# A hybrid decoder layer on one core: the output projection of the first 512 tokens between the SSD's chunks

## The chip, the cores and the metric

The kernel runs on one core of a Trainium2 chip. The core has TensorE (matmuls and transposes, "PE" in the rows, its weight loads "PEld"), VectorE ("DVE"), ScalarE ("ACT"), GpSimd ("POOL") and SyncE ("SP"), which issues the DMAs. Each engine works through its own queue in order and waits on semaphores for the others. The metric is the device time of one execution, in microseconds, as the median of several runs.

## The reference

One layer of a decoder for a prompt of 2048 tokens and, with the same weights, 32 sample tokens (8 sequences of 4). The input projection feeds four parallel groups of 256 channels each, whose normed outputs are concatenated, projected and added to x; then comes a feed-forward block.

```python
xn = rmsnorm(x, P['norm_mix_g'][l])
u, q, k, v, fr, z, xbc, dtr, sb, sc, sh = split_cols(xn @ P['w_in'][l])
ya, h_s5n = s5_mix(u, ...)                                    # diagonal state-space model
yb = fox_prompt(q, k, v, logf)                                # attention, 4 heads of 64
yc, h_ssdn, buf_ssdn = ssd_mix(z, xbc, dtr, ...)              # chunks of 128 tokens
yd, buf_scn = short_conv_mix(sb, sc, sh, buf_sc, P['sc_conv_w'][l])
# ya, yb, yc, yd each go through rmsnorm
x = x + jnp.concatenate([ya, yb, yc, yd], axis=-1) @ P['w_out'][l]
hn = rmsnorm(x, P['norm_ffn_g'][l])
x = x + jnp.square(jax.nn.relu(hn @ P['w_up'][l])) @ P['w_down'][l]
```

The shapes are `D_MODEL` 1024, `SEQ` 2048, `FFN_WIDTH` 4096; outputs are y, the keys, values and states of both groups.

## The kernel before, in words

Prompt tokens are handled in 16 tiles of 128 and 4 blocks of 512. Numbers that need more than 16 bits are held as a high and a low half (`w[:, k, 0]`, `w[:, k, 1]`), so that one product of 128 tokens with 256 columns is 8 x 3 = 24 matmuls (`proj_tok`), accumulated in PSUM.

The stages are traced by `run`. `phase_in` norms and projects the input and runs the S5, the short convolution and the sample's attention. Then come the SSD (`ssd`), the attention of the prompt (`fox`), the output projection (`outproj`) and the feed-forward block (`ffn`). A scheduler orders the instructions of each engine by priority and readiness; `priority(bg)` places attention ahead of the SSD (`priority(first)`), and both ahead of `outproj`, so a stage of lower priority fills the gaps of a higher one. A wait between stages follows from which tile was traced as written before which read.

Attention works by query block j (512 tokens) and head h: `maxima` runs ahead and finds row maxima (scores into a PSUM bank, `mx` on VectorE at L871); `attend` goes through 4j + 4 key blocks: two score matmuls, the exponential on ScalarE (`P`, L902), its high half `ph` (ScalarE or VectorE), its low half `pl` (GpSimd, L909), and 12 matmuls with `v`. A head ends with `fo_o` (VectorE, L920). After four heads `fox_out` norms the block's four tiles: a square on ScalarE, a power on GpSimd, a scale on ScalarE, two transposes on TensorE, a split into `fo_cat`, a DMA into the DRAM buffer `catD[1][j]`. It uses PSUM tag `b` (5 banks).

The SSD goes through 16 chunks: `prepare` (decay matrix `sE`, transposes, `G`), `advance` (products into `y`, state `shT`, gate `syo`), then `fox_out` of the chunk before into `catD[2]`. It uses tag `x` (the 2 banks named `px`) and tag `d` (1 bank, `pd`). Between chunks the sample's SSD (`sample`) goes on by one step, and `w_out` prepares one quarter of the output weights in chunks 10, 12, 13 and 14: a 1 MB load, a square pass (L183) and a high half (L176) on ScalarE, a low half (L177) on VectorE, and the scale between them.

`outproj` uses `px` for products and `pd` for transposes. It takes tokens 0 to 511 (block 0), 512 to 1023, then blocks 2 and 3. For each half block it loads `cat` (the four groups) and `x2` (the input), runs 8 products of 512 columns, adds each in two halves (L1908), norms the sum (`norm_pair`), and for blocks 0 and 1 stores the sum to `xD` and the normed parts to `hD` in DRAM; the FFN reads these back later. The sample's 32 tokens go through `out_sample` (192 matmuls `px<-catS,w`) after the first half block. Its tiles lie in pools that are opened after the SSD's pools are closed.

Of the kernel before, what the change touches and what calls it, by code (L numbers as in the profile page):

```python
# [9 lines left out]
F32 = mybir.dt.float32  # L10
F16 = mybir.dt.float16
# [3 lines left out]
OP = mybir.AluOpType  # L15
# [4 lines left out]
D = 1024  # L20
# [7 lines left out]
BLOCKS = [(2, 3), (0, 1)]  # L28
FC = 256
# [74 lines left out]
class K:  # L104
# [131 lines left out]
    def run(self):  # L236
        tc = self.tc
        with ExitStack() as ctx:
# [9 lines left out]
            self.wp = ctx.enter_context(self.pool("wp", 4))  # L248
            first = tc.cur_priority
            tc.cur_priority = first + 50000  # L250
            if "ssd" in self.stages:
                with self.priority(first), self.banks(t="x", s="x", o="d"), ExitStack() as c3:
                    self.mark("ssd")
                    self.ssd(c3)
            if "fox" in self.stages:
                with self.priority(bg):
                    self.mark("fox")
                    self.fox(mix)
            if getattr(self, "dump", None):
                self.dump_cat()  # L260
# [786 lines left out]
    def ssd_prompt(self, ctx, Dp, av, sample):  # L1047
# [109 lines left out]

        hT, yo = None, None
        self.Wo, wo = [], self.w_out()
        nx = prepare(0)  # L1160
        for i in range(NT):
            cur, nx = nx, prepare(i + 1) if i + 1 < NT else None
            old = yo
            hT, yo = advance(i, hT, *cur)

            if old is not None:
                self.fox_out(p2, old, 128, i - 1, "t", 2)
            next(sample, None)
            if i in (10, 12, 13, 14):
                next(wo)  # L1170
        for _ in sample:
            pass
# [703 lines left out]

    def outproj(self, ctx, mix):

        nc, A = self.nc, self.A
# [7 lines left out]

        self.xD = {b: [self.dr.tile([128, 2 * D], F32, name=f"x2D{b}{i}") for i in range(2)] for b in BLOCKS[1]}
# [21 lines left out]
        for b in BLOCKS[1]:  # L1910
            hns = [rot.tile([128, 7, 4, 2, N2[b]], F16, name="hnr") for _ in range(2)]
            for i, hn in enumerate(hns):
                cat, x2 = load(2 * b + i, BLOCKS[0][0], i)
                for t in range(2):
                    for m in (0, 2):
                        product(cat, x2, t, m)
                self.norm_pair(x2, gb, hn[:, :, :, :, 0:128])
                if i == 0 and N2[b] > 128:
                    self.out_sample(g8, [h[:, :, :, :, 128:] for h in hns])
                nc.sync.dma_start(self.xD[b][i], x2.rearrange("p t d -> p (t d)"))  # L1920
                nc.sync.dma_start(self.hD[b][i], hn.rearrange("p o k a n -> p (o k a n)"))
# [396 lines left out]
```

## Time and profile before

| | us |
|---|---|
| median of 3 runs (lowest, highest) | 2579.73 (2573.97, 2580.62) |
| the profiled execution | 2576.48 |
| its span, first to last instruction | 2574.7 |
| TensorE busy in the span | 2422.8 |
| VectorE busy | 1855.7 |
| ScalarE busy | 1209.2 |
| GpSimd busy | 980.4 |

A row of the trace gives an instruction's start and length on its engine; the idle time before it is put down to what ended it. Matmuls are pipelined, so each is shown longer than the distance to the next one; the pace is read from a run of them. The granted clock is the mean of TensorE's clock over a stretch, as a share of 2.4 GHz; the clock has that level and 1.2 GHz. Attention runs from about 740 to 1132 us, the SSD beside it from about 840 to 1030 us, and the feed-forward block from about 1290 us to the end.

### The profile page before, as it was taken

What the parts mean: (1) busy time and instruction counts of PE and PEld (TensorE: products, weight loads), DVE (VectorE), ACT (ScalarE), POOL (GpSimd) and SP (SyncE); (2) the same over time, 40 slices, a digit from 0 to 9 for tenths busy, and PEclk for the clock granted to TensorE, in tenths of its full rate; (3) what the DMA queues carried; (4) which work ended last, traced back from release to release, by engine and by line L of the source; (5) the groups of instructions that cost most, each with busy time, mean ns of one, the idle gap of its engine ahead of it and who ended that gap; (6) DMA issues with size and microseconds to landing.
All of it is one profiled execution on the core that took longest, in us unless ns stands there. A gap on an engine that the chain in (4) does not pass through costs nothing.

```text
span 2574.7 us, 51102 instructions
## 1 busy us (share of the span) xinstructions
PE 2422.8 (94%) x20496; PEld 1655.2 (64%) x20496; DVE 1855.7 (72%) x3636; ACT 1209.2 (47%) x2339; POOL 980.4 (38%) x1141
## 2 busy tenths in 40 slices
PE   7989998999999899999969999999999999999996
PEld 6975554444467677689846666666666666666663
DVE  7566667875576777655579898888886776777765
ACT  6434333033346677653455556555554333333333
POOL 3403121223124566651165555555534222222222
PEclk9999999999999998999979999999999999999998
DMA  6333415869732433347233443435466232232221
GB/s 178 100 76 95 90 41 194 306 245 345 239 110 81 134 97 103 103 147 248 79 122 133 147 172 143 156 138 178 156 260 234 107 123 84 101 123 104 81 78 68
DMA packets 201864, 368.42 MB, mean 143 GB/s; under 512 B 43829, under 2 KB 161714, under 8 KB 179322
## 3 DMA queue, kind: packets, MB, share of 16 engines
q1 hardware_dynamic: 187594, 293.29, 34.4%
q0 software_dynamic: 9376, 67.64, 7.2%
q10 hardware_dynamic: 4656, 4.23, 0.5%
q8 instruction: 160, 2.62, 0.4%
q14 instruction: 78, 0.64, 0.1%
HBM read 245.87 MB, written 116.39 MB: 141 GB/s over the span
## 4 chain that ended last, share of the span: by engine, by line
PE 63%; DVE 11%; POOL 8%; DMA 8%; ACT 4%; issue 4%; SPq 2%; POOLq 0%; DVEq 0%; ACTq 0%
PE pb L140 30%; PE px L140 28%; DMA ws<-in_w_up_dram 3%; PE pd L140 2%; DVE x L2203 2%; DVE wu L177 2%; PE pb L144 1%; DMA kp<-in_cache_v_dram,ptV 1%; ACT wdT L176 1%; POOL ht L2159 1%; DVE s5cat L480 1%; POOL ht L2157 1%; DVE wd L177 1%; PE pd L144 1%; POOL fr L2149 1%
## 5 line engine op out<-in xcount | busy, mean ns | idle before, releaser
L2203 DVE SCALAR_TENSOR_TENSOR x<-pb,ff,x 128x512 f32<-128x512 f32 x840 | 593.6, 744 | 107.0 <-PE pb L140 101.4
L140 PEld LDWEIGHTS <-wu 128*128 128x128 f16 x5376 | 524.6, 98 | 192.3 <-issue 20.0
L140 PE MATMUL px<-hn,wu 128*128 128x256 f16 (+1 forms) x3072 | 414.5, 275 | 12.3 <-DVE hn L1983 7.0
L140 PEld LDWEIGHTS <-ht 128*128 128x128 f16 x2712 | 263.7, 98 | 242.8 <-issue 23.4
L140 PE MATMUL pb<-wdT,ht 128*128 128x512 f16 x1440 | 378.9, 380 | 10.1 <-DVE x L2203 5.0
L140 PE MATMUL px<-xT,w 128*128 128x512 f16 (+1 forms) x1968 | 369.3, 339 | 1.5 <-ACT da L731 1.2
L140 PE MATMUL pb<-wd,ht 128*128 128x512 f16 x1272 | 330.0, 380 | 10.5 <-DVE x L2203 10.2
L140 PE MATMUL pb<-hn,wu 128*128 128x256 f16 (+1 forms) x2304 | 305.4, 276 | 6.5 <-ACT hn L1982 4.7
L140 PEld LDWEIGHTS <-w 128*128 128x128 f16 x2160 | 170.2, 99 | 188.0 <-issue 27.5
L2157 POOL TENSOR_TENSOR ht<-fr,ht 128x512 f16<-128x512 f32 (+1 forms) x60 | 80.8, 1347 | 402.7 <-ACT ht L2156 401.7
L909 POOL TENSOR_TENSOR pl<-P,ph 128x512 f16<-128x512 f32 (+3 forms) x160 | 166.8, 1052 | 154.3 <-ACT ph L906 64.8
L140 PE MATMUL px<-w,cat 128*128 128x256 f16 x1536 | 175.9, 273 | 3.0 <-DMA cat<-cat 3.0
L140 PE MATMUL px<-w,xT 128*128 128x128 f16 (+1 forms) x2400 | 158.9, 227 | 8.9 <-DVE v L576 3.3
L140 PEld LDWEIGHTS <-xT 128*128 128x128 f16 (+1 forms) x2672 | 155.8, 102 | 14.4 <-issue 4.2
L140 PEld LDWEIGHTS <-cat 128*128 128x128 f16 x1536 | 149.2, 98 | 22.7 <-DMA cat<-cat 3.1
L2131 ACT ACTIVATE fr<-fr 128x256 f32<-128x256 f32 (+1 forms) x192 | 78.0, 416 | 153.8 <-DVE fr L2112 152.4
L902 ACT ACTIVATE P<-pb,nck,cc 128x512 f32<-128x512 f32 (+3 forms) x160 | 113.0, 713 | 73.2 <-PE pb L140 67.5
L2154 ACT ACTIVATE ht<-fr 128x1024 f16<-128x1024 f32 (+1 forms) x60 | 64.2, 1070 | 137.6 <-POOL fr L2160 137.6
L871 DVE TENSOR_REDUCE mx<-pb 128x1 f32<-128x512 f32 (+3 forms) x160 | 94.8, 607 | 38.0 <-PE pb L140 36.6
L2132 ACT ACTIVATE fr<-fr 128x256 f32<-128x256 f32 (+1 forms) x256 | 104.1, 416 | 5.1
L177 DVE SCALAR_TENSOR_TENSOR wu<-ws,wsc,wu 128x1024 f16<-128x1024 f32 x64 | 91.2, 1432 | 13.3 <-ACT wu L176 13.1
L176 ACT ACTIVATE wu<-ws,wsc 128x1024 f16<-128x1024 f32 x64 | 64.8, 1039 | 64.9 <-POOL ws L2045 37.6
(717 smaller groups left out, 4196.0 us busy)
## 6 DMA issues: line engine op xcount, KB each, us to landing
w0D<-wu SPq DMA_DIRECT2D x16, 1792.0 KB
wu<-w0D SPq DMA_DIRECT2D x16, 1792.0 KB
ws<-in_w_up_dram SPq DMA_DIRECT2D x16, 1024.0 KB
ws<-in_w_down_dram SPq DMA_DIRECT2D x16, 1024.0 KB
w1D<-wd SPq DMA_DIRECT2D x16, 1024.0 KB
wd<-w1D SPq DMA_DIRECT2D x16, 1024.0 KB
w2D<-wdT SPq DMA_DIRECT2D x15, 1024.0 KB
wdT<-w2D SPq DMA_DIRECT2D x15, 1024.0 KB
```

The costliest lines, as they stand in the source:

```text
L140: self.nc.tensor.matmul(out, lhsT, rhs, start=start, stop=stop, skip_group_check=True)
L144: self.nc.tensor.transpose(out, in_, self.ident[:n, :n])
L176: self.nc.scalar.activation(hi, x, AF.Copy, scale=sc)
L177: self.nc.vector.scalar_tensor_tensor(lo, x, sc, hi, op0=OP.mult, op1=OP.subtract)
L871: nc.vector.tensor_reduce(mx[:, ii, jb:jb + 1], s[:, :n], axis=AX.X, op=OP.max)
L902: nc.scalar.activation(P[:, :n], s[:, :n], AF.Exp, bias=nck[:, j, h, kt:kt + 1], scale=cc[:, h // 2:h // 2 + 1])
L909: (nc.gpsimd if 1 else nc.vector).tensor_sub(pl[:, :n], P[:, :n], ph[:, :n])
L2131: nc.scalar.activation(x, x, AF.Relu)
L2132: nc.scalar.activation(x, x, AF.Square)
L2154: nc.scalar.activation(ht[:, o:o + m, 0, :], x, AF.Copy)
L2157: nc.gpsimd.tensor_sub(ht[:, 0:2, 1, :], C[:, 0:2, :], ht[:, 0:2, 0, :])
L2203: nc.vector.scalar_tensor_tensor(o, p, f, o, op0=OP.mult, op1=OP.add)
```

## The change

- `fox` is traced ahead of `ssd`; their priorities stay. So the SSD's loop can read `catD[1][0]`, attention's output for block 0.
- `w_out` runs in chunks 1 to 4.
- `out_tile(EARLY, t)` is the output projection of one tile of 128 tokens of block 0: it loads `ecat` and `ex2` (pool `eo`, two buffers), runs four products of 256 columns in the SSD's `px` banks, adds each into `ex2`, and stores the sum to `xD`. From chunk 6 on, two of these 16 quarters are traced behind each chunk.
- `outproj` skips the products of block 0 and reads the sum back from `xD` for the norm.

```diff
--- before.py
+++ after.py
@@ -26,6 +26,7 @@
 BIG = float(2.0 ** 100)
 S14 = float(2.0 ** -14)
 BLOCKS = [(2, 3), (0, 1)]
+EARLY = 0
 FC = 256
 PLAIN = ((0, 15), (1, 15))
 V_EARLY, V_LAG = 12, 4
@@ -246,16 +247,19 @@
                 bg = self.phase_in(c2)
             self.wst = ctx.enter_context(self.pool("wst", 2))
             self.wp = ctx.enter_context(self.pool("wp", 4))
+
+            self.xD = {b: [self.dr.tile([128, 2 * D], F32, name=f"x2D{b}{i}") for i in range(2)] for b in BLOCKS[1]}
             first = tc.cur_priority
             tc.cur_priority = first + 50000
-            if "ssd" in self.stages:
-                with self.priority(first), self.banks(t="x", s="x", o="d"), ExitStack() as c3:
-                    self.mark("ssd")
-                    self.ssd(c3)
             if "fox" in self.stages:
                 with self.priority(bg):
                     self.mark("fox")
                     self.fox(mix)
+            if "ssd" in self.stages:
+                with self.priority(first), self.banks(t="x", s="x", o="d"), ExitStack() as c3:
+                    self.mark("ssd")
+                    self.eo = c3.enter_context(self.pool("eo", 2))
+                    self.ssd(c3)
             if getattr(self, "dump", None):
                 self.dump_cat()
             with self.banks(mm="x", t="d"):
@@ -1155,6 +1159,7 @@
                 nc.gpsimd.tensor_mul(yo, yt, z)
             return hN, yo
 
+        early = (s for t in range(4) for s in self.out_tile(EARLY, t))
         hT, yo = None, None
         self.Wo, wo = [], self.w_out()
         nx = prepare(0)
@@ -1166,9 +1171,14 @@
             if old is not None:
                 self.fox_out(p2, old, 128, i - 1, "t", 2)
             next(sample, None)
-            if i in (10, 12, 13, 14):
+            if 1 <= i < 5:
                 next(wo)
+            if i > 5:
+                for _ in range(2):
+                    next(early, None)
         for _ in sample:
+            pass
+        for _ in early:
             pass
         self.fox_out(p2, yo, 128, NT - 1, "t", 2)
         t = self.ps("t", [128, 2, 128])
@@ -1874,6 +1884,23 @@
             self.Wo.append((w, f))
             yield
 
+    def out_tile(self, b, t):
+
+        nc, A, W = self.nc, self.A, self.Wo
+        cat = self.eo.tile([128, 8, 2, 128], F16, name="ecat")
+        for g in range(4):
+            nc.sync.dma_start(cat[:, 2 * g:2 * g + 2], self.catD[g][b][:, :, :, t * 128:t * 128 + 128])
+        x2 = self.eo.tile([128, D], F32, name="ex2")
+        r = (4 * b + t) * 128
+        nc.sync.dma_start(x2, A["x_prompt"][0, r:r + 128, :])
+        for m in range(4):
+            p = self.ps("t", [128, 256])
+            self.proj_tok(p, cat, W[m][0], 0, 256)
+            o = x2[:, m * 256:(m + 1) * 256]
+            nc.vector.scalar_tensor_tensor(o, p, W[m][1], o, op0=OP.mult, op1=OP.add)
+            yield
+        nc.sync.dma_start(self.xD[b][t // 2][:, t % 2 * D:t % 2 * D + D], x2)
+
     def outproj(self, ctx, mix):
 
         nc, A = self.nc, self.A
@@ -1884,8 +1911,6 @@
 
         self.xp = {BLOCKS[0][0]: ctx.enter_context(self.pool("x2a", 1))}
         rot = mix.enter_context(self.pool("rot", 2, "right"))
-
-        self.xD = {b: [self.dr.tile([128, 2 * D], F32, name=f"x2D{b}{i}") for i in range(2)] for b in BLOCKS[1]}
         N2 = {BLOCKS[1][0]: 128 + NS // 4, BLOCKS[1][1]: 128}
         self.hD = {b: [self.dr.tile([128, 7 * 4 * 2 * N2[b]], F16, name=f"hnD{b}{i}") for i in range(2)] for b in BLOCKS[1]}
 
@@ -1910,14 +1935,18 @@
         for b in BLOCKS[1]:
             hns = [rot.tile([128, 7, 4, 2, N2[b]], F16, name="hnr") for _ in range(2)]
             for i, hn in enumerate(hns):
-                cat, x2 = load(2 * b + i, BLOCKS[0][0], i)
-                for t in range(2):
-                    for m in (0, 2):
-                        product(cat, x2, t, m)
+                if b == EARLY:
+                    x2 = self.xp[BLOCKS[0][0]].tile([128, 2, D], F32, name="x2", tag=f"x2{BLOCKS[0][0]}{i}")
+                    nc.sync.dma_start(x2.rearrange("p t d -> p (t d)"), self.xD[b][i])
+                else:
+                    cat, x2 = load(2 * b + i, BLOCKS[0][0], i)
+                    for t in range(2):
+                        for m in (0, 2):
+                            product(cat, x2, t, m)
+                    nc.sync.dma_start(self.xD[b][i], x2.rearrange("p t d -> p (t d)"))
                 self.norm_pair(x2, gb, hn[:, :, :, :, 0:128])
                 if i == 0 and N2[b] > 128:
                     self.out_sample(g8, [h[:, :, :, :, 128:] for h in hns])
-                nc.sync.dma_start(self.xD[b][i], x2.rearrange("p t d -> p (t d)"))
                 nc.sync.dma_start(self.hD[b][i], hn.rearrange("p o k a n -> p (o k a n)"))
         first = [load(2 * BLOCKS[0][0] + i, BLOCKS[0][0], i) for i in range(2)]
         for i, t, m in ((i, t, m) for i in range(2) for t in range(2) for m in (0, 2)):
```

How this moves TensorE's queue: of the 1536 matmuls `px<-w,cat` of the prompt's output projection, 240 stand ahead of attention's last matmul in the kernel before and 1296 behind it; in the changed kernel 384 (now with `ecat`) stand ahead and 1152 behind. The 192 small ones of the sample (`px<-catS,w`) stand ahead of it before and behind it now. The SSD's chunks, which in the kernel before end with head (3, 0), now reach to attention's end; heads (2, 1) to (3, 0) hold ten chunks before and six now, heads (3, 1) to (3, 3) none before and four now.

TensorE at the end of attention, before (the matmuls with `v` and `pl` are attention's; `os` is the sample's sum of squares, `w,cat` the projection):

```order
L140 MATMUL pb<-v_3_11130,ph 128x64
L140 MATMUL pd<-os,ones 128x32 x3
L140 LDWEIGHTS pl
L140 MATMUL pb<-v_3_11130,pl 128x65
L140 LDWEIGHTS cat
L140 MATMUL px<-w,cat 128x256
```

and now (`sXd,sBt` is the state of the last chunk, `fo_on` a norm's transposes, `fn_sq`, `fn_rs` the sample's norm, `shT` the final state, `catS,w` the sample's projection):

```order
L141 MATMUL pb<-v_3_9840,ph 128x64
L141 LDWEIGHTS pl
L141 MATMUL pb<-v_3_9840,pl 128x65
L141 MATMUL px<-sXd,sBt 128x128
L145 MATMUL px<-cst,fo_on 128x128 x2
L141 MATMUL px<-ones,fn_sq_16255 32x1 x2
L141 MATMUL px<-cst,fn_rs 128x32
L145 MATMUL px<-cst,fo_on 128x128 x2
L145 MATMUL px<-cst,shT 128x128 x2
L145 MATMUL pb<-cst,fo_on 128x128 x2
L141 LDWEIGHTS w
L141 MATMUL px<-catS,w 128x32
```

The projection behind attention's last matmul has given way to the last SSD chunk's and the norms' transposes.

VectorE between the ends of heads (1, 3) and (2, 0), before:

```order
L871 TENSOR_REDUCE mx<-pb 128x1
L908 CAST ph<-P 128x512
L871 TENSOR_REDUCE mx<-pb 128x1
L1115 TENSOR_TENSOR sX<-px,dt 128x256
L1152 TENSOR_TENSOR syt<-pd,acu 128x256
L871 TENSOR_REDUCE mx<-pb 128x1
L1154 TENSOR_TENSOR syt<-syt,pd 128x256
L871 TENSOR_REDUCE mx<-pb 128x1
L874 TENSOR_REDUCE nm<-mx 128x4
L1125 TENSOR_TENSOR sE<-sE,px 128x512
L875 TENSOR_SCALAR nm<-nm,sh 128x4
L908 CAST ph<-P 128x512
```

and now (`w<-ws,w_sc,w` is the low half of a quarter of w_out, `w_f` to `wo_f` the scales):

```order
L188 TENSOR_SCALAR w_f<-pd 128x1
L875 TENSOR_REDUCE mx<-pb 128x1
L156 TENSOR_SCALAR w_m<-w_f 128x1
L1119 TENSOR_TENSOR sX<-px,dt 128x256
L192 TENSOR_SCALAR w_sc<-w_m 128x1
L178 SCALAR_TENSOR_TENSOR w<-ws,w_sc,w 128x8x256
L193 RECIPROCAL w_inv<-w_sc 128x1
L875 TENSOR_REDUCE mx<-pb 128x1
L1129 TENSOR_TENSOR sE<-sE,px 128x512
L912 CAST ph<-P 128x512
L1883 TENSOR_TENSOR wo_f<-w_inv,isc 128x1
L875 TENSOR_REDUCE mx<-pb 128x1
```

Between the ends of heads (1, 2) and (2, 0) there are four such halves now and none before, and 28 of the maxima `mx<-pb` where there were 24.

SP from the second load of w_out on, before:

```order
L160 DMA ws<-in_w_out_dram 128x8x256
L857 DMA q_12681<-qk_2912 64x512
L848 DMA kbm<-kb 74x512
L848 DMA kba<-kb 74x512
L857 DMA q_12681<-qk_2912 64x512
L858 DMA q_12682<-qk_2912 64x512
L859 DMA q_12682<-row 10x512
```

and now:

```order
L161 DMA ws<-in_w_out_dram 128x8x256
L1892 DMA ecat<-cat_0_117 128x4x128
L1892 DMA ecat<-cat_0_121 128x4x128
L1892 DMA ecat<-cat_0_129 128x4x128
L1895 DMA ex_15190<-in_x_prompt_dram 128x1024
L1892 DMA ecat<-cat_0_117 128x4x128
L1892 DMA ecat<-cat_0_121 128x4x128
L852 DMA kba<-kb 74x512
L852 DMA kbm<-kb 74x512
```

Six loads of `ecat` and `ex2` stand ahead of attention's `kba` and `kbm`.

## Rows read from the trace of the kernel before

**Rows 1.** Busy time by engine, share of the span, instructions (the page).

```profile
PE 2422.8 (94%) x20496; PEld 1655.2 (64%) x20496; DVE 1855.7 (72%) x3636; ACT 1209.2 (47%) x2339; POOL 980.4 (38%) x1141
```

**Rows 2.** Stretches: length, busy us (instructions) by engine, granted clock, DMA share, GB/s.

```profile
785.90:848.90 63.00, 56.27 (x802) 44.59 (x799) 40.73 (x99) 43.99 (x100) 28.69 (x34) 0.95 0.36 103
848.90:909.10 60.20, 55.65 (x544) 41.44 (x543) 45.66 (x105) 41.66 (x102) 38.26 (x59) 1.00 0.43 124
909.10:987.20 78.10, 76.88 (x839) 58.59 (x837) 63.59 (x138) 57.10 (x115) 55.80 (x69) 1.00 0.37 106
987.20:1044.10 56.90, 50.94 (x435) 37.27 (x435) 41.21 (x99) 40.67 (x87) 36.49 (x46) 0.82 0.26 71
1044.10:1132.20 88.10, 82.55 (x1154) 64.26 (x1153) 49.68 (x94) 56.63 (x94) 54.77 (x52) 0.98 0.35 107
1132.20:1283.00 150.80, 150.80 (x1384) 136.23 (x1382) 80.55 (x138) 58.17 (x95) 27.48 (x38) 1.00 0.51 178
1283.00:1335.00 52.00, 29.60 (x220) 23.86 (x218) 41.13 (x46) 33.13 (x52) 30.98 (x25) 0.80 0.34 127
```

**Rows 3.** Timeline of VectorE, ends of heads: start, us, line, operation, tiles.

```profile
909.11 0.42 DVE L920 TENSOR_TENSOR fo_o<-pb,rl 128x256 f32<-128x256 f32 x1
...
987.22 0.41 DVE L920 TENSOR_TENSOR fo_o<-pb,rl 128x256 f32<-128x256 f32 x1
...
1044.14 0.42 DVE L920 TENSOR_TENSOR fo_o<-pb,rl 128x256 f32<-128x256 f32 x1
```

**Rows 4.** Chain of waits after attention, timeline of TensorE inside it: start, us, count.

```profile
1203.85 33.41 PE px L140 x306
...
1107.38 0.45 PE L140 MATMUL px<-catS,w 128*128 128x32 f16 x12
```

**Rows 5.** Groups: busy us, mean ns, idle before; three of 987.2:1044.1, last 760:1160.

```profile
L176 ACT ACTIVATE w<-ws,w_sc 128x2048 f16<-128x2048 f32 x3 | 6.0, 2013 | 0.0
...
L183 ACT ACTIVATE w<-ws 128x2048 f16<-128x2048 f32 x1 | 1.9, 1903 | 0.0
...
L177 DVE SCALAR_TENSOR_TENSOR w<-ws,w_sc,w 128x2048 f16<-128x2048 f32 x3 | 7.0, 2344 | 0.0
...
L871 DVE TENSOR_REDUCE mx<-pb 128x1 f32<-128x512 f32 (+3 forms) x146 | 88.6, 621 | 37.6 <-PE pb L140 36.3
```

**Rows 6.** Waits of TensorE in 987.2:1044.1: us in total, times, longest us.

```profile
PE pb L144 <- ACT fo_on L959: 3.4, 2, 2.6
```

**Rows 7.** Waits of TensorE in 1044.1:1132.2.

```profile
PE px L140 <- DMA cat<-cat: 3.0, 1, 3.0
PE pb L140 <- DMA kba<-kb: 2.5, 2, 2.1
```

**Rows 8.** Timeline, steps of a chunk's norm; the last row is another chunk's.

```profile
1009.97 0.42 DVE L1152 TENSOR_TENSOR syt<-pd,acu 128x256 f32<-128x256 f32 x1 [1.29 <-PE pd L140]
...
1010.43 0.42 DVE L1154 TENSOR_TENSOR syt<-syt,pd 128x256 f32<-128x256 f32 x1
...
1014.35 0.42 ACT L956 ACTIVATE fo_on<-syo 128x256 f32<-128x256 f32 x1
...
1014.65 0.21 ACT L956 ACTIVATION_READ_ACCUMULATOR fo_on<-syo 128x1 f32 x1
...
1014.95 0.19 POOL L150 TENSOR_SCALAR fo_rs<-fo_ssq 128x1 f32<-128x1 f32 x1
...
1015.99 0.56 POOL L151 TENSOR_TENSOR fo_rs<-fo_rs,mhalf 128x1 f32<-128x1 f32 x1
...
1016.70 0.54 ACT L959 ACTIVATE fo_on<-syo,fo_rs 128x256 f32<-128x256 f32 x1
...
1028.50 0.91 POOL L1155 TENSOR_TENSOR syo<-syt,sz 128x256 f32<-128x256 f32 x1
```

**Rows 9.** Timeline of SP, issues around the first w_out loads.

```profile
837.73 0.39 SPq L160 DMA_DIRECT2D ws<-in_w_out_dram  x1
843.76 0.48 SPq L857 DMA_DIRECT2D q<-qk  x1
```

## The prediction

> **What bounds the kernel now.** I read the busy shares first, then stretches cut at the places where attention finishes a head (the write of `fo_o`, L920), then the waits inside them. TensorE is busy 94% of the span [rows 1], so the first question about any change of this kind is whether TensorE does less work or waits less. The stretches [rows 2] are cut at heads [rows 3]: with (j, h) for query block j and head h, 785.9 to 848.9 is (1,0) to (1,2); 848.9 to 909.1 is (1,3) and (2,0); 909.1 to 987.2 is (2,1) to (2,3); 987.2 to 1044.1 is (3,0) alone; 1044.1 to 1132.2 is (3,1) to (3,3). From 1132.2 to 1283.0 only output projection is left, and TensorE is busy 150.80 of 150.80 us, at full clock. From 1283.0 to 1335.0 it waits for the last norm and the first FFN weights (29.60 of 52.0 us).
>
> Output projection runs at the pace of its columns: 306 matmuls follow each other in 33.41 us, 0.109 us each [rows 4]. The plain reading of the change would be that 384 of these (42 us) leave the full stretch after attention. The order denies it. In the kernel before, 240 projection matmuls and all 192 small ones of the sample tokens already stand between attention's matmuls, in its last three heads, after the SSD has ended; in the changed kernel 384 stand there and the 192 small ones come after it. TensorE's work in the attention stage therefore hardly changes, and what matters is where it waits.
>
> It waits mostly in one place. In (3,0) TensorE's records fill 50.94 of 56.9 us, but at a granted clock of 0.82 [rows 2]: the mean of the 1.2 and 2.4 GHz levels, so 0.18 x 56.9 = 10.2 us are given away, and the same work takes about 40.7 us at the full clock. (3,0) thus loses 16 us. Three of the four w_out splits stand there on VectorE (7.0 us) and four 2 us passes on ScalarE [rows 5], and TensorE waited for attention's norm, 3.4 us in two waits [rows 6]; no single wait accounts for the 16 us. By comparison (2,1) to (2,3) loses 78.1 - 76.88 = 1.2 us at clock 1.00, and (3,1) to (3,3) 88.1 - 82.55 = 5.6 us plus 0.02 x 88.1 = 1.8 us of clock, mostly waits for `cat` and `kba` (5.5 us, [rows 7]).
>
> **The change part by part.**
>
> *w_out in chunks 1 to 4.* Its four splits now stand on VectorE between the ends of heads (1,2) and (2,0), where none stood, and five of its ScalarE passes with them; four more maxima (L871) are drawn there too. VectorE's work in 848.9 to 909.1 becomes 45.66 + 4 x 2.35 + 4 x 0.62 = 57.5 us, ScalarE's 41.66 + 5 x 1.96 = 51.5, TensorE's about 57 [rows 2, 5]. Six SSD chunks stand there before and after. Three engines then need 51 to 58 us in a stretch that lasts 60.2. How much longer it gets the trace doesn't show; it is bounded by the factor between the longest engine's work and the time in two stretches: 60.2/55.65 = 1.08 there, and 56.9/41.21 = 1.38 in (3,0), where the same splits stood. That is 62 to 79 us, +2 to +19. I take 68 (**+8**), nearer the lower end, because attention in this stretch has 12 blocks to (3,0)'s 16 and TensorE's clock there is 1.00.
>
> *Heads (2,1) to (3,0).* They lose the splits and four of ten SSD chunks, and gain 240 projection matmuls, 26.2 us. A chunk costs TensorE some 5 us, an estimate: (2,1) to (2,3) hold seven and 76.88 us, of which three heads at the (82.55 - 26.2 - 5)/3 = 17 us of j = 3, scaled by 12/16 blocks, take 38. TensorE's work goes from 76.9 + 40.7 = 117.6 to about 122 us. At the occupancy of the stretch that already mixes heads with projection (88.1/82.55 = 1.067) it takes 130, without any wait 122. I take 127 for the 135.0 of now, **-8**; the bounds are -13 and 0, the latter if the waits stay although the splits are gone. The products use the two banks `px` that the SSD uses; each needs VectorE's add (L1908) before the bank is free again, and what queues behind a late add is the next SSD transpose. Projection in these banks ran beside attention with TensorE's only waits being for DMAs [rows 7], so I charge nothing more.
>
> *Heads (3,1) to (3,3).* 96 projection matmuls (10.5 us), the small ones and the norm transposes leave, four SSD chunks (20 us) come. Near even: **-1**, between -5 and +3. The loads of `ecat` and the stores to `x2D` stand in SP's queue between attention's `kba` and `kbm`, and an `ecat` load waits for TensorE to finish the tile before; `kba` waits have cost 2.5 us already [rows 7], hence the +3.
>
> *The end of attention.* Before, the matmul after attention's last one is a projection matmul that waits for nothing. In the changed kernel SSD chunk 15 ends with attention, and TensorE stands in front of the transposes of two SSD norms, the sample's norm, the final state and attention's own norm, then of the small matmuls that need the sample's norm. Nothing else is ahead of these, as the projection's pools lie where the SSD's lay and their loads wait for its end. The chain of one chunk from its last matmul to its transposes is 0.42 + 0.42 + 0.91 + 0.42 + 0.21 + 0.19 + 0.56 + 0.54 = 3.7 us of bare work, and took 7.3 us where the engines had other work (1009.97 to 1017.24) [rows 8]. Behind it attention's own chain adds ScalarE and GpSimd steps of the same kind, some 2 us. After that the 192 small matmuls (0.025 us each: 12 in 0.45 us less the 0.18 of the last, [rows 4]) hide 4.8 us of the reading back of `x2` and the load of `cat`, and the sample's `x2_s` load stands in SP's queue behind one that waits for the norm. I take 4 + 2 + 2 = **+8**, bounds 4 and 12, the upper one with a fall of the clock as in (3,0).
>
> *After attention.* 144 matmuls (15.7 us) fewer; the small ones (4.8), the norm transposes and sums of tokens 0 to 255 (about 7) and the last SSD transposes (1) come there: **-2.5**. The rest, from the projection of tokens 512 on, stands in the same order as before. *Early loads.* Five `ecat` loads and one `ex2` go ahead of `kba` and `kbm` on SP. SP sat idle from 838.1 to 843.8 [rows 9], which hides their issue; behind two 1 MB loads their 1.2 MB may delay `kba` a little: **+1**, 0 to 3. The adds, loads of x and stores are the same in number or lie off the path.
>
> The sum is 8 - 8 - 1 + 8 - 2.5 + 1 = +5.5 us. Against the profiled execution (2574.7 span, 2576.48 us) that is 2582.0; against the median of the runs, which stands 3.25 above it, 2585.2. I forecast **2584 us**.
>
> **A page that speaks against it.** In the trace projection, attention and one `px` ring together kept the clock at 0.98 in 1044.1 to 1132.2, and SSD with attention at 1.00 in 909.1 to 987.2 [rows 2]. The Trainium skill ("TensorE: Matmul & The Clock Gate", A second HAM failure mode: psum-queue depth-cycling) tells of a kernel that cycles through PSUM banks in each iteration, leaves TensorE briefly idle between groups, and so swings between its clock levels. By that, products and SSD sharing two banks would bring the clock of (3,0) to all heads behind it; the trace so far disagrees.
>
> **The rivals.** *Faster: the waits of (3,0) go and little comes back.* For it speaks that the splits were the only thing special to (3,0) and that six heads then have dense work to fill gaps. With +2 for the first stretch, -13, -3, +4, -2.5 and 0 it gives -12.5, **2567 us**. Against it: the splits land in a stretch whose three engines are all nearly full.
>
> *Slower: the stretch of the splits becomes a second (3,0).* Its place is (1,3) to (2,0); its price 57.5 x 1.38 = 79 us, +19, with the other terms +17 in all, **2597 us**. It decides once ScalarE's and VectorE's queues keep attention's exponentials back for longer than the two or three score blocks TensorE has ahead, and the clock falls. For it speaks that (3,0) did just that with three splits; against, that its lost clock came with the j = 2 norms as well.
>
> *Slower by the clock.* If the shared banks keep the clock at 0.82, the 122 + 80 us of work in (2,1) to (3,3) take 246 us instead of 214, **2616 us**.
>
> *The change moves its full 384 matmuls out of the stretch behind attention.* Then 42 us go, **2538 us**; the count in the order is against it.
>
> **How the numbers follow.** A measurement of this kernel tells about 0.3% (7.7 us) from no change. Forecast 0.45, faster rival 0.20, second (3,0) 0.27, the clock 0.05, the full gain 0.03. Faster than 2572: 0.20 + 0.03 = 0.23. Slower than 2587.5: 0.27 + 0.05 and 0.03 of the forecast's own upper edge, 0.35. Within: 0.42. The range takes in both larger rivals and stops short of the last two: 2565 to 2602.
>
> **What would show it.** The profile after should have the time from (1,3) to the end of (2,0) near 68 us with VectorE at some 57; a clock near 1.00 in (3,0) and a length of 44 to 48 us; a hole of 5 to 8 us on TensorE right behind attention's last matmul, ended by ScalarE's `fo_on` or VectorE's `catS`; and 1283 to 1335 repeated unchanged. It is wrong if the hole is missing, if (3,0) keeps its clock of 0.82 without splits, or if the products wait for VectorE's adds.

## The result, and the profile after

The changed kernel takes 2593.18 us (median of 6 runs, 2591.07 to 2601.16), the kernel before 2576.39 us beside it (6 runs): 1.0073 times the time, 95% interval 1.0058 to 1.0088, slower by more than the 0.3% that can be told from no change. The profiled execution took 2592.22 us with a span of 2590.1.

The busy row of the page after, to be read against [rows 1]:

```profile
PE 2426.3 (94%) x20496; PEld 1652.8 (64%) x20496; DVE 1853.0 (72%) x3636; ACT 1209.8 (47%) x2339; POOL 979.7 (38%) x1141
```

Every engine does what it did before (TensorE 3.5 us more), so the 15.4 us between the spans are waits and clock (a matmul at the lower level counts as busy for longer: `px<-w,cat` takes 273 ns at the median here, 421 where the clock is 0.50). The stretches of after, cut at the same heads as [rows 2] (length, busy us of PE, PEld, DVE, ACT, POOL, granted clock, DMA share, GB/s):

```profile
847.60:924.10 76.50, 66.18 (x586) 46.06 (x585) 59.78 (x130) 55.10 (x113) 50.95 (x63) 0.91 0.47 139
924.10:1042.50 118.40, 117.22 (x1270) 89.96 (x1267) 78.03 (x174) 74.08 (x152) 69.64 (x88) 1.00 0.35 100
1042.50:1128.80 86.30, 85.73 (x1016) 65.18 (x1014) 47.36 (x105) 59.66 (x113) 59.83 (x68) 0.98 0.14 42
1128.80:1172.00 43.20, 26.95 (x332) 21.41 (x330) 19.72 (x44) 17.89 (x42) 7.33 (x17) 0.76 0.66 212
1172.00:1298.60 126.60, 126.60 (x1163) 114.47 (x1163) 74.50 (x123) 51.10 (x74) 24.03 (x28) 1.00 0.48 175
1298.60:1350.00 51.40, 29.46 (x217) 23.65 (x215) 41.52 (x46) 33.79 (x54) 31.58 (x25) 0.80 0.37 139
```

Call the first three A ((1,3) and (2,0)), B ((2,1) to (3,0)) and C ((3,1) to (3,3)). A grew from 60.2 to 76.5 us, B fell from 135.0 to 118.4, C from 88.1 to 86.3. A and B together last 194.9 us, where they lasted 195.2. B is all but full now: 117.22 us of TensorE in 118.4 at clock 1.00. Behind attention a full stretch has given way to 43.2 us in which TensorE is busy for 26.95, at a clock of 0.76. Its waits in 1128.8 to 1175 (us in total, times, longest):

```profile
PE pd L145 <- DVE xn L1993: 6.9, 1, 6.9
PE pd L145 <- DMA x_s<-in_x_sample_dram: 2.3, 1, 2.3
PE px L141 <- DMA cat<-cat: 2.1, 1, 2.1
PE pd L145 <- ACT xt L1998: 2.1, 3, 0.7
PE px L141 <- POOL fn_rs L1023: 1.8, 1, 1.8
```

The longest can be followed through three timelines (SP, ScalarE, TensorE; start, us, line, tiles, idle time before it and what ended that):

```profile
1137.87 3.29 SPq L1921 DMA_DIRECT2D cat<-cat  x3
...
1143.31 1.04 SPq L1940 DMA_DIRECT2D x<-x2D  x2
...
1150.66 1.06 ACT L1990 ACTIVATE xn<-x 128x1024 f32<-128x1024 f32 x1 [4.52 <-DMA x<-x2D]
...
1154.09 1.12 PE L145 MATMUL pd<-cst,xn 128*128 128x128 f32 x4 [6.94 <-DVE xn L1993]
```

SP issued the read-back of block 0's sum at 1143.31, 14.5 us behind attention's end and behind the first loads of `cat`; it landed at 1150.7, and TensorE stood before the norm's transposes until 1154.09, with products of tokens 512 on queued behind them. Right behind attention, up to the first product, TensorE was idle for only 2.1 us:

```profile
1128.80:1139.00 10.20, 8.13 (x210) 7.19 (x208) 5.52 (x18) 6.80 (x24) 4.15 (x11) 0.83 0.63 155
```

The table gives the stages of every kernel that ran, from its profiled execution: A, B, C; "end" from attention's last `fo_o` to the first matmul of the feed-forward block (the first that reads `hn`); "sum" of these four; "FFN" from there to the span's end; and the ratio of its runs to those of before.

| kernel | A | B | C | end | sum | FFN | ratio, 95% interval |
|---|---|---|---|---|---|---|---|
| before | 60.2 | 135.0 | 88.1 | 152.4 | 435.7 | 1290.1 | |
| after | 76.5 | 118.4 | 86.3 | 170.9 | 452.1 | 1290.4 | 1.0073, 1.0058 to 1.0088 |
| e1_traced_first | 60.7 | 134.4 | 88.6 | 152.4 | 436.1 | 1290.1 | 0.9998, 0.9989 to 1.0008 |
| e2_splits_spread | 77.2 | 121.1 | 86.2 | 174.3 | 458.8 | 1303.7 | 1.0138, 1.0122 to 1.0155 |
| e3_splits_alone | 71.5 | 125.0 | 92.2 | 152.4 | 441.1 | 1302.0 | 1.0046, 1.0029 to 1.0063 |
| e4_norm_later | 78.2 | 118.4 | 84.6 | 164.2 | 445.4 | 1290.6 | 1.0049, 1.0035 to 1.0063 |
| e5_later_products | 78.1 | 113.7 | 87.0 | 171.8 | 450.6 | 1301.6 | 1.0084, 1.0054 to 1.0115 |
| e6_quarter_passes | 78.1 | 124.5 | 92.9 | 161.3 | 456.8 | 1293.2 | 1.0061, 1.0043 to 1.0080 |
| e9_before_quarter | 62.1 | 136.2 | 100.1 | 142.5 | 440.9 | 1293.3 | 1.0050, 1.0027 to 1.0073 |
| e10_loads_held | 69.5 | 124.7 | 84.6 | 170.1 | 448.9 | 1301.0 | 1.0099, 1.0083 to 1.0115 |
| e11_half_early | 78.1 | 118.0 | 89.4 | 154.0 | 439.5 | 1301.9 | 1.0057, 1.0042 to 1.0071 |
| e12_half_held | 69.4 | 126.9 | 99.1 | 139.3 | 434.7 | 1292.9 | 1.0007, 0.9995 to 1.0019 |
| e13_half_const | 68.9 | 125.8 | 97.5 | 146.5 | 438.7 | 1308.1 | 1.0066, 1.0045 to 1.0086 |
| e14_before_const | 69.1 | 131.5 | 93.0 | 152.4 | 446.0 | 1294.7 | 1.0030, 1.0015 to 1.0044 |

The whole loss of the changed kernel lies in the sum (452.1 - 435.7 = 16.4 us); its feed-forward block is that of before. In six experiments that block took 1301 us or more without an edit of its own, so the sums are compared below, not the totals. A sum is from one execution: the kernel before and e1, whose queues are the same, differ by 0.5 us in A; the changed kernel and e4, where TensorE's queue is the same up to attention's end, by 1.7.

### The profile page after: what moved, and what is told of

The parts are those of the page before. It is cut to its first block, busy times and chain, and to the rows that moved or that the text cites. A ratio compares the mean times of both kernels' runs of the same rounds, so it can differ in the third digit from the quotient of the medians.

```text
span 2590.1 us, 51110 instructions
## 1 busy us (share of the span) xinstructions
PE 2426.3 (94%) x20496; PEld 1652.8 (64%) x20496; DVE 1853.0 (72%) x3636; ACT 1209.8 (47%) x2339; POOL 979.7 (38%) x1141
## 4 chain that ended last, share of the span: by engine, by line
PE 60%; DVE 10%; DMA 10%; POOL 8%; ACT 5%; issue 5%; SPq 2%; POOLq 0%; DVEq 0%; ACTq 0%
PE pb L141 29%; PE px L141 26%; DMA ws<-in_w_up_dram 4%; PE pd L141 2%; DVE x L2232 1%; DVE wu L178 1%; PE pb L145 1%; DMA kp<-in_cache_v_dram,ptV 1%; DMA ws<-in_w_down_dram 1%; POOL ht L2186 1%; POOL ht L2188 1%; PE pd L145 1%; DVE s5cat L484 1%; ACT wdT L177 1%; POOL fr L2178 1%
## 5 line engine op out<-in xcount | busy, mean ns | idle before, releaser
L141 PE MATMUL pb<-wd,ht 128*128 128x512 f16 x1272 | 330.0, 380 | 10.3 <-DVE x L2232 10.3
L141 PE MATMUL px<-w,cat 128*128 128x256 f16 x1152 | 131.3, 275 | 2.9 <-DMA cat<-cat 2.1
L141 PEld LDWEIGHTS <-cat 128*128 128x128 f16 x1152 | 113.4, 99 | 17.7 <-DMA cat<-cat 3.0
```

The source lines that it names most:

```text
L141: self.nc.tensor.matmul(out, lhsT, rhs, start=start, stop=stop, skip_group_check=True)
```

## The experiments

**The order of tracing alone.** The two stages are exchanged in `run`, nothing else.

> The kernel before, with attention traced ahead of the SSD and nothing else. If what the changed kernel gains and loses comes from the splits of w_out and from the products, as I read it, this one repeats the kernel before: within 5 us of it, head (3,0) near 57 us, (1,3) with (2,0) near 60, and no hole behind attention. If the order of tracing by itself sets it, part of the gain in (2,1) to (3,0) (16.6 us) or of the loss behind attention (19 us) is here already, and the time differs by more than 8 us.

Ratio 0.9998 and a sum of 436.1: the first theory. Every engine's queue is, instruction for instruction, that of before.

**Where the gain in B comes from.** The kernel before with the splits moved:

```diff
-            if i in (10, 12, 13, 14):
+            if 1 <= i < 5:
```

> The kernel before with w_out prepared in chunks 1 to 4; no early products, the SSD traced first as before. If the splits cost where they stand, (1,3) with (2,0) becomes about 76 us (+16) and (3,0) falls from 57 to 41 to 46 us, so that the total comes out within 5 us of before: the move of the splits would be even, and the gain of 16.6 us in (2,1) to (3,0) would be theirs, not the products'. If the gain in (3,0) comes from the products that fill TensorE's gaps, (3,0) stays above 52 here and the total is 10 to 16 us above before.

(3,0), and A, in this kernel:

```profile
855.10:926.60 71.50, 64.12 (x551) 47.26 (x550) 55.78 (x131) 52.39 (x111) 48.73 (x64) 0.86 0.46 134
...
1006.00:1051.60 45.60, 42.25 (x387) 30.98 (x386) 32.31 (x79) 31.01 (x76) 28.92 (x40) 0.89 0.23 61
```

(3,0) falls from 56.9 to 45.6, as the first theory had it. A rises by 11.3, less than the 16 expected, and B falls by 10.0: over A and B the move of the splits is nearly even, and 10.0 of B's 16.6 us are the splits'. The other 6.6 are not the products': e10 below has the products, and its B is 124.7, near the 125.0 of this kernel. C rises by 4.1 here and falls by 1.8 in the changed kernel; it holds other work there (SSD chunks for products), so this is no price of either. The sum is 5.4 us above that of before, and the feed-forward block takes 11.9 us more, so the total (1.0046, some 12 us) missed its expectation.

**Why A is long.** First the splits further apart:

```diff
-            if 1 <= i < 5:
+            if i in (1, 3, 5, 7):
```

> The changed kernel with the four quarters of w_out prepared in chunks 1, 3, 5 and 7 instead of 1 to 4. If four splits close together make (1,3) and (2,0) 16 us longer, two of them there cost about 8 and the other two, in heads with spare VectorE time, little: (1,3) with (2,0) near 68 us, (2,1) to (3,0) up to 4 us longer than the 118.4 of the changed kernel, in all 4 to 8 us below it, 2585 to 2589. If instead the stretch is long because the SSD's chunks and the products' loads crowd there, it stays at 76 and the time does not move (2593).

A stayed at 77.2 us with two splits in it, not four, and VectorE at 52.04 us. So the sum of VectorE's work is not what sets it. The time, 2613.74 us, fits neither theory: the sum is 6.7 us longer and the feed-forward block 13.3. A whole, and then cut at its pauses, reads in this kernel:

```profile
847.30:924.50 77.20, 68.02 (x545) 49.16 (x544) 52.04 (x116) 48.15 (x105) 43.43 (x59) 0.82 0.45 135
...
847.30:861.30 14.00, 10.00 (x119) 6.23 (x118) 7.74 (x16) 7.63 (x15) 6.54 (x7) 1.00 0.71 217
861.30:873.30 12.00, 11.21 (x48) 8.18 (x47) 6.74 (x15) 4.01 (x12) 3.98 (x9) 0.57 0.19 54
873.30:889.30 16.00, 14.16 (x119) 11.02 (x118) 13.29 (x33) 14.00 (x36) 12.60 (x18) 1.00 0.54 164
889.30:897.30 8.00, 8.00 (x45) 5.26 (x45) 3.57 (x11) 5.59 (x10) 2.26 (x4) 0.58 0.58 163
897.30:905.30 8.00, 5.51 (x68) 4.31 (x66) 7.20 (x17) 7.16 (x12) 7.37 (x8) 1.00 0.27 64
905.30:917.30 12.00, 12.00 (x82) 8.76 (x82) 7.28 (x14) 5.46 (x11) 5.61 (x7) 0.57 0.34 107
```

Three times TensorE is idle for 1.8 to 4 us in a stretch (10.00 us busy of 14.00, 14.16 of 16.00, 5.51 of 8.00), and each time the 8 to 12 us behind it run at 0.57 or 0.58, mostly the 1.2 GHz level. So each pause here cost its own length and clock behind it. Over all of A the clock is 0.82, and 0.18 x 77.2 = 13.9 us is the most that this can have cost. A's length does not follow its clock from kernel to kernel, though: it is 71.5 us at 0.86 in e3 and 69.5 at 0.95 in e10 (shown below).

Next, the same work in shorter passes, in the changed kernel and in the one before (in a copy of `wprep` for `w_out` alone; the square and its column sum are cut in four likewise):

```diff
-        self.split(w[:, :, 0, :], w[:, :, 1, :], st, sc)
+        for q in range(4):
+            x = slice(2 * q, 2 * q + 2)
+            self.split(w[:, x, 0, :], w[:, x, 1, :], st[:, x], sc)
```

> The changed kernel with the square, the high half and the low half of each quarter of w_out made in four passes of a quarter each (about 0.6 us on VectorE and 0.6 us on ScalarE instead of 2.35 and 2.0), the same work in sum and some fixed cost more. If (1,3) and (2,0) take 76.5 us because attention's short steps stand behind passes of 2 us and TensorE runs dry and loses its clock, that stretch falls to 62 to 68 us and the total to 2579 to 2586. If the loads of w_out on the DMA queues or the sum of work on VectorE and ScalarE make it long, it stays at 74 to 78 us and the total at 2590 to 2596.

> The kernel before, with the passes of w_out in quarters as in e6_quarter_passes and nothing else. If the length of the passes holds attention up, head (3,0) falls from 56.9 us at a clock of 0.82 to 45 to 49 us near full clock, and the total comes out 7 to 12 us below before (2568 to 2573). If it is the amount of work, (3,0) stays at 55 to 58 us and the total within 3 us of before.

A is 78.1 us in the one and (3,0) is 55.9 us in the other: attention standing behind a pass of 2 us is not the cause (on VectorE the four passes of a low half took 0.8 us each on average). The totals are not better for it either: 1.0061, and 1.0050 (some 13 us) where no more than 3 us were expected. In both, C is longer and the end shorter than without the edit, the sums are some 5 us longer, and why is open. Then the loads that the products bring:

```diff
         cat = self.eo.tile([128, 8, 2, 128], F16, name="ecat")
+        nc.gpsimd.tensor_copy(cat[:, :, 0, 0], self.yo[:, 0:8])
...
         x2 = self.eo.tile([128, D], F32, name="ex2")
+        nc.gpsimd.tensor_copy(x2[:, 0:1], self.yo[:, 0:1])
```

> The changed kernel with the loads of ecat and ex2 held back: GpSimd first writes a few elements of each tile from the gate output of the SSD chunk behind which the products are traced, so no load can go ahead of that chunk. In the changed kernel SP issued six of these loads from 837.3 to 844.5 us and two more at 853.6, and the first RL load of the SSD, which before stands 3.2 us behind the sxbc load, came 5.8 us behind it. If (1,3) with (2,0) takes 76.5 us partly for that, it falls to the 70 to 72 of e3_splits_alone, which has the splits and no early products. If the splits alone make it, it stays at 75 to 78 us. The FFN's queue stands in another order here (as in e2 and e3, worth some 12 us), so the stages are to be compared: from the end of (1,2) to the first FFN matmul 452 us in the changed kernel, 445 to 447 here by the first theory, 451 to 453 by the second.

SP of the changed kernel, against [rows 9], from the loads of `w_out` to the SSD's first `RL`:

```profile
836.85 0.39 SPq L161 DMA_DIRECT2D ws<-in_w_out_dram  x1
837.29 4.49 SPq L1892 DMA_DIRECT2D ecat<-cat  x3
841.82 1.45 SPq L1895 DMA_DIRECT2D ex<-in_x_prompt_dram  x1
843.32 1.20 SPq L1892 DMA_DIRECT2D ecat<-cat  x2
...
853.64 0.56 SPq L1892 DMA_DIRECT2D ecat<-cat  x1
854.25 0.62 SPq L1895 DMA_DIRECT2D ex<-in_x_prompt_dram  x1
...
856.03 1.64 SPq L1108 DMA_DIRECT2D RL<-acD  x1
```

Six loads took SP 7.1 us, and two more stood ahead of `RL`. With the loads held back, the stretches A and B (in two), and TensorE's longest waits in A, are:

```profile
851.90:921.40 69.50, 60.52 (x562) 45.41 (x561) 55.99 (x131) 52.56 (x111) 48.78 (x64) 0.95 0.46 138
921.40:999.50 78.10, 77.83 (x863) 58.22 (x861) 51.67 (x113) 46.90 (x89) 45.46 (x56) 1.00 0.31 87
999.50:1046.10 46.60, 45.01 (x467) 34.75 (x466) 30.45 (x69) 32.00 (x73) 29.19 (x44) 1.00 0.47 132
```

```profile
PE pb L141 <- POOL pl L913: 2.6, 2, 1.4
PE pd L141 <- ACT w L184: 2.3, 1, 2.3
PE pd L141 <- DVE w_f L188: 1.5, 2, 1.2
```

A falls by 7.0 us to 69.5, just under the 70 to 72 expected, near e3's 71.5 without any products. But B grows by 6.3, and A and B together last 194.2 us, where they lasted 194.9. The same pair stands in e11 (early loads) and e12 (held), 196.1 and 196.3. So the early loads make A longer and B shorter by the same amount. Part of that is only where the cut lies, a write of VectorE's: with the early loads 80 of attention's matmuls with `pl` stand ahead of it, with the loads held 68, as in the kernel before. Windows of the changed kernel and of e10, of the instructions on `pl` alone (TensorE, its loads, GpSimd):

```profile
847.60:924.10 76.50, 9.98 (x80) 8.05 (x80) 26.13 (x23) 0.91 0.47 139
851.90:921.40 69.50, 8.18 (x68) 6.61 (x68) 22.45 (x20) 0.95 0.46 138
```

The sum falls by 3.2 us, between the two theories, and 2.5 of these are in C and the end. Held loads change both SP's order and the traffic while the SSD starts, and the two are not told apart. A is still 9.3 us longer than before, by the splits.

Of those 9.3, the waits for `w` and `w_f` belong to the scale (a square on ScalarE, a column sum that stands in TensorE's queue until the square is done, short steps behind it). Two kernels set a constant scale and leave these steps out:

```diff
...
+            self.nc.vector.memset(sc, 1024.0)
+            self.nc.vector.memset(inv, 1.0 / 1024)
+            self.split(w[:, :, 0, :], w[:, :, 1, :], st, sc)
```

> The kernel before with the scale of w_out set to a constant power of two instead of worked out: it leaves out the square pass on ScalarE, the column sum on TensorE in the bank pd, and the short steps on VectorE and GpSimd behind it. The loads, the high and the low halves stay (2.0 and 2.35 us, four times). With nothing to wait for but their loads, the four low halves now stand in (1,3). If what the splits cost (11 us, wherever they stood) is the chain from ScalarE over TensorE's queue and the one bank pd to VectorE and GpSimd, it is gone: (1,3) with (2,0) stays at 60 to 63 us, (3,0) falls to 45 to 47 as in e3_splits_alone, and the total to 2566 to 2572. If the passes on VectorE and ScalarE themselves cost it, (1,3) with (2,0) becomes 68 to 72, (3,0) falls all the same, and the total is within 5 us of before.

> e12_half_held with the constant scale of e14_before_const (it leaves out the same steps). By the theory of the chain (1,3) with (2,0) falls from 69.4 us to 60 to 63 and the stages from the end of (1,2) to the first FFN matmul from 434.7 to 425 to 429 us. By the theory of the passes it stays at 67 to 70 and the stages at 432 to 436. The FFN's queue stands in another order here, so the total is no measure of the two.

A is 69.1 and 68.9 us, (3,0) 47.4 and 44.0, as the theory of the passes said; e14's total is 5.6 us above before and e13's sum 438.7, both just above what it allowed. But it is no proof of it. In e14 the longest wait is another one, and a fall of the clock to 0.86 goes with it:

```profile
845.00:914.10 69.10, 59.27 (x506) 43.24 (x504) 51.28 (x103) 45.05 (x95) 40.53 (x52) 0.86 0.42 122
```

```profile
PE pd L140 <- DMA sxbc<-xbc: 4.8, 1, 4.8
```

The splits came earlier there (the low halves from 848.5 to 871.1 us), and the SSD's first load, issued 1.2 us ahead of A in the kernel before, came 6.2 us into it. The splits cost about 9 to 11 us in A wherever they stood in it, through whichever wait came to be the longest; what makes it just that much stays open.

**The hole behind attention.** First the norm of block 0 goes behind the products of block 1:

```diff
-        for b in BLOCKS[1]:
+        for b in BLOCKS[1][::-1]:
```

> The changed kernel with block 1 (tokens 512 to 1023) projected ahead of the norm of block 0 in the output projection, so that the read-back of the sum and its norm no longer stand in TensorE's queue ahead of the first products. If that norm makes the hole behind attention (43 us with 27 us of TensorE work and a clock of 0.76), TensorE starts on products as soon as cat lands and 10 to 15 us come back: 2578 to 2583. If the hole comes from the SSD's last chunk, its norms and the loads of cat that wait for them, it stays, and the time is 2590 to 2595.

The two stretches from attention's end to the last product, and TensorE's longest waits in the first 48 us of them:

```profile
1131.90:1142.00 10.10, 4.17 (x19) 1.96 (x19) 5.24 (x16) 6.73 (x24) 4.17 (x11) 0.64 0.66 161
1142.00:1294.10 152.10, 148.13 (x1466) 132.31 (x1466) 88.21 (x148) 61.34 (x91) 26.81 (x34) 0.97 0.56 196
```

```profile
PE pb L145 <- ACT fo_on L963: 2.6, 3, 1.8
PE px L141 <- POOL fn_rs L1023: 1.8, 1, 1.8
PE px L141 <- DMA cat<-cat: 1.6, 1, 1.6
```

The end falls by 6.7 us to 164.2, and the ratio from 1.0073 to 1.0049 (2590.70 us beside 2581.39 for the kernel before). That is less than the 10 to 15 expected: behind attention 10.1 us with 4.17 of work at a clock of 0.64 remain, in which TensorE waits for the last norms (`fo_on`, `fn_rs`) and for `cat`. Next, products kept for that gap, by taking one quarter behind each chunk and the rest behind the SSD:

```diff
-                for _ in range(2):
-                    next(early, None)
+                next(early, None)
...
```

> The changed kernel with block 1 projected ahead of block 0's norm (as in e4_norm_later), one early quarter behind each chunk instead of two, and the rest of them behind the SSD's last step, so that 42 of the 384 early matmuls stand behind attention's last one. In e4_norm_later TensorE was busy 4.2 of the 10.1 us between the end of attention and the first product. If that hole is only a lack of ready work while the SSD's last norms and the loads of cat go on, the 4.6 us of early products fill it and the stretch from attention's end to the first FFN matmul falls from 164 to about 159 us. If the loads of cat, which cannot start before the SSD's tiles are free, are what ends last, they start later by the same time and the stretch stays at 164 or grows. The FFN's queue stands in another order here than in the changed kernel (as it did in e2 and e3, where the FFN took 1302 to 1304 us instead of 1290), so the total is expected some 12 us above that, 2590 to 2600, and the stages are to be compared, not the total.

The end is 171.8 us, and the first product comes 13.7 us behind attention: what opens when the SSD's tiles are free only opens later. TensorE's longest wait there, 5.8 us, is for a step on the norm's gain, whose load also waits for those tiles.

```profile
PE px L141 <- DVE gr_m L156: 5.8, 1, 5.8
```

Last, half of block 0 early, without and with the loads held back:

```diff
-        early = (s for t in range(4) for s in self.out_tile(EARLY, t))
+        early = (s for t in range(2) for s in self.out_tile(EARLY, t))
...
-                if b == EARLY:
+                if b == EARLY and i == 0:
```

> The changed kernel with two of block 0's four tiles projected early; the other half block goes through the old path with its own loads and products. The SSD then ends in (3,2) instead of with attention, so the projection's tiles come free and its loads run while attention still goes on. If the loss of 19 us behind attention comes from the SSD ending with attention (its last norms, then loads that cannot start before its tiles are free, then a norm at the head of the queue), it goes: from attention's end to the first FFN matmul 150 to 154 us instead of 171, and 434 to 440 us instead of 452 from the end of (1,2). If it comes from the products having moved out of that stretch, so that less work covers the loads there, at least half of it stays (160 or more). The FFN's order is that of e2 and e3, so the total is some 12 us above what the stages give: 2585 to 2592.

> e11_half_early and e10_loads_held together, with the FFN's queue in the order of the kernel before. By the theory that the loss is made of early loads ahead of the SSD's first chunks (5 us) and of the SSD ending with attention (17 us), while the gain of 15 to 18 us in (2,1) to (3,3) is the products' and the splits', (1,3) with (2,0) is 70 to 72 us, (2,1) to (3,3) 204 to 212, and the end as before: 2565 to 2576 us, a little faster than before or the same. By the theory that the products cost elsewhere what they save, 2580 or more.

Attention's end to the last product, in e11 and then e12:

```profile
1138.70:1290.70 152.00, 151.69 (x1391) 136.63 (x1390) 86.22 (x148) 61.13 (x99) 29.84 (x38) 1.00 0.51 177
```

```profile
1147.90:1285.10 137.20, 136.83 (x1254) 123.39 (x1252) 74.55 (x113) 55.66 (x87) 22.47 (x35) 1.00 0.54 187
```

The hole is gone in both: TensorE is busy 151.69 us of 152.00 and 136.83 of 137.20, at clock 1.00. e11 alone would not tell the two theories apart, since most of the work is back behind attention there (1275 projection matmuls against 1152 in the changed kernel, 1289 before). e12 does: it has 1163, hardly more than the changed kernel, and no hole. So a lack of work behind attention did not make it. e11's end is 154.0 us, at the edge of the 150 to 154 expected, its sum 439.5 against 452.1; its time, 2594.25 us, is 2 us above the range. SP issues the read-back of the sum in e12 59 us ahead of attention's end:

```profile
1088.98 0.35 SPq L1943 DMA_DIRECT2D x<-x2D  x1
```

Of the kernels with 1152 products behind attention and the norm ahead of them, this moment is 14.7 us behind attention's end in e2, 14.5 in the changed kernel, 9.8 in e10 and 3.7 in e6, and the end lasts 174.3, 170.9, 170.1 and 161.3 us. Where it lies ahead of attention's end (e11, e12, e13), the stretch is full and as long as its work. e10 adds that an earlier end of the SSD is not enough by itself: its first load of `cat` goes out 1.7 us ahead of attention's end (5.3 behind it in the changed kernel), but the read-back stands behind eight of these loads, and TensorE waits 9.8 us for the norm:

```profile
PE pd L145 <- DVE xn L1996: 9.8, 1, 9.8
```

In e12 both repairs hold, A 69.4 and the sum 434.7, and the total, 2582.03 us, is that of before (1.0007, 0.9995 to 1.0019): the theory that the products cost elsewhere what they save. B and C together take 226.0 us, not the 204 to 212 expected: once the SSD has ended, 181 projection matmuls and the 192 small ones stand in C beside attention (247 and 192 before), and the heads last longer by that work while the end gets shorter. None of the kernels beats before.

## Why the prediction came out as it did

The time lies in the range (2565 to 2602), 9 us above the forecast of 2584, and it is slower, which had 0.35, not the same, which had 0.42. As a change it is three times what was forecast: +16.8 us of the medians, +5.5 in the sum of terms. The first two terms cancel as the text said, at twice their size; the third is right; the whole loss comes from the end of attention, where the text had the place and the cause right and the step that costs most wrong. That 2593 is in the range owes as much to the range's width as to the terms.

- *w_out in chunks 1 to 4 (+8; measured +16.3).* VectorE's work was right (59.78 us for 57.5). The splits' own price is near what was taken: 9.3 us in e10, 11.3 in e3. The other 7.0 us come with the early loads and come back in B (6.3). In A and B together the early loads cost 0.7 us, and 3.2 in the sum, against the +1 (0 to 3) of the text: about right, although two loads stood ahead of the SSD's first `RL`, which the text did not see.
- *Heads (2,1) to (3,0) (-8; measured -16.6).* Beyond the bound of -13. Without the part that A takes over it is the -10.3 of e10. The bound let TensorE's work grow to 122 us without any wait; it was 117.22, and 122.84 in e10. The clock of 1.00 and (3,0)'s 45.5 us came as described, and the products did not wait for VectorE's adds.
- *(3,1) to (3,3) (-1; measured -1.8).* Right. The `kba` waits that it feared did not grow.
- *The end of attention and after (+8 - 2.5; measured 170.9 - 152.4 = +18.5).* The text put 4 + 2 us on the norms' chain right behind attention's last matmul; up to the first product TensorE was idle for 2.1 us there. It put 2 us on the reading back, as the 192 small matmuls "hide 4.8 us of the reading back of `x2` and the load of `cat`". This is the step that failed: the loads' place in SP's queue was not followed, the read-back was issued 14.5 us behind attention's end, and 14.2 of the hole's 43.20 - 26.95 = 16.25 idle us lie behind the first product. The norm that the read-back feeds cost 6.7 us of this (e4). The fall of the clock stood only in the upper bound: 6.85 us of TensorE's work ran at 0.50, 6.00 at 0.76, 8.13 at 0.83, some 6 us given away, an estimate. With the work that left (its terms add to -2.9, not -2.5) that is 16.25 + 6 - 2.9, about 19 us. That the SSD's end lets the loads start only then was in the text, and e11 and e12 show it: with the SSD ended earlier the hole is gone.
- *From 1283 on, unchanged.* Right: 29.46 of 51.40 us against 29.60 of 52.0 in [rows 2], and the same feed-forward block.

The sign that the text named came in part: a hole, but 43 us long and ended by the norm's `xn`, not by `fo_on` or `catS`.

Of the rivals, the second (3,0) came nearest (79 us for A, 2597 in all), but its reason isn't borne out: neither less VectorE work in A (e2) nor shorter passes (e6) shortened it, and 7.0 us of A came back in B. The rival of the clock, with its sentence on the Trainium skill ("TensorE: Matmul & The Clock Gate", A second HAM failure mode: psum-queue depth-cycling), did not come about: with SSD and products on the same two banks beside attention, the clock was 1.00 over 118.4 us. The brief idling that the page names was missing too, as TensorE was busy for 117.22 us of these, so this run does not test the page. The clock fell after pauses: TensorE was busy for 0.01 us of the 6.90 before 1154.1, and the clock was 0.50 from there to 1166.

## What to carry to other kernels

Work that is moved into a gap brings its loads along, and a load that waits for nothing is issued as early as the queue allows: hold it back, or look at what it now stands ahead of. Before a stage is stretched to the end of the one beside it, ask what opens when it closes, tiles and pools included, and where in the queue the load stands that the next product waits for; that comes late by the same time, and the clock of 0.50 behind the pause comes on top. Before a stage is called longer, look at its neighbour and at what lies on either side of the cut: here 7.0 us of one came back as 6.3 in the other. Compare stages, not totals, where a scheduler may reorder what lies behind the edit.

## What was not expected

- The feed-forward block took 1290.1 to 1294.7 us in eight kernels and 1301.0 to 1308.1 in six, none of which edits it. TensorE's queue in that block holds over 2100 matmuls in other places in each of those six, and some 40 at most in the others (none in e1, e4, e6, e9 and e12). The scheduler fixes this order when the kernel is built, and edits upstream changed it. With the other order the block is 11 to 18 us longer than before's, as much as anything the change did; no run changes the order alone.
- Executions whose queues are the same up to the loads of `w_out` (some 837 us) end the first head anywhere between 754.4 us (after) and 762.0 (e9). Totals of single executions differ by this much without a cause in the edit.
